# Expert pass of a two-layer trunk: two groups of 32 slots without a branch and the third under a condition, in place of one of four arms

## The chip, the cores and the metric

One core of a Trainium2 chip runs the whole program. The metric is the time of one execution on the device in microseconds (us).

## The reference

The reference is a trunk of two layers over 256 tokens of width 1024, all in float32. Each layer has a mixer (convolution and spatial gating) and a feed-forward part. The feed-forward part of layer 0 is dense; that of layer 1 sends every token to two of eight experts, and it is there that the change is made:

```python
def swiglu(h, wg, wu, wd):
    return jnp.einsum('...f,fd->...d', jax.nn.silu(h @ wg) * (h @ wu), wd)

def moe_swiglu(h, router, wg, wu, wd):
    ...
    top_vals, top_idx = lax.top_k(logits, TOP_K)
    gates = jax.nn.softmax(top_vals, axis=-1)
    ...
    for e in range(N_EXPERTS):
        out = out + dense_gate[:, e:e + 1] * swiglu(ht, wg[e], wu[e], wd[e])
```

`h` is 256 x 1024, and each expert has `wg` and `wu` of 1024 x 2816 and `wd` of 2816 x 1024. A final RMS norm follows.

## The kernel before

**Stages.** `mixer(0)`, `dense`, `mixer(1)` and `moe` run one after the other; `moe` begins at about 393 us of the profiled execution. The routing is worked out at the end of `mixer(1)`: `rt.pos` holds for every token and expert its place among that expert's tokens (a large negative number where it is not sent there), `rt.icnt` the number of tokens of each expert.

**Slots.** An expert's tokens are gathered into slots, 128 in the main pass, in groups of `GW` = 32 (`NG` = 4). `one_hot` (L1184) compares `pos` with 0 to 127 for a pair of experts. `gather` (L1208) multiplies the normalised tokens `xn` by this one-hot matrix, so that `xg` has the chosen tokens as columns, for two experts at once. If an expert has more than 128 tokens, the whole pass is run once more (`second_half`, L1470) under a condition at the end (L1523), then with all four groups; in this execution it is not run.

**Sections.** Each expert's 2816 hidden columns are cut into three blocks: two of 1024 and one of 768. For each block `hidden` (L1264) computes gate and up projection, and `down` (L1327) multiplies by the rows of `wd`. A section is one call of `hidden` or `down`; `experts` (L1374) puts them in this order for expert e: hidden 0, down 2 of expert e-1, hidden 1, down 0, hidden 2, down 1. Between them stand `turn` (L1300: transposes of the hidden values into `ah`), `back` (L1341: transposes of the one-hot matrix into `pt`), `combine` (L1355: copies of `mpd` to `eo`, the products `pcomb` that bring slots back to tokens, and eight additions to `xs` on VectorE), and, after every second expert, the gather for the next pair.

**Matmuls of a section.** `side_by_side` (L1249) puts four matmuls beside each other on TensorE: the 32 slots of a group are the stationary operand, and four column ranges of the weights stream past them into four quarters of the PSUM partitions. All of L1253 in the profile is this function. A float32 matmul shows as two MATMUL and two LDWEIGHTS instructions. One group is 128 of these MATMUL instructions of 256 columns in hidden 0 and in hidden 1, 192 of 128 columns in hidden 2, 64 of 256 columns in down 0 and in down 1, and 48 in down 2.

**Branches.** How many groups an expert needs is known at run time only. `arms` (L1228) writes every section out four times, for one to four groups, and two nested conditions choose (L1233, L1234, L1239). The count `c` is loaded into a register of TensorE once for each expert (L1516). The instructions of the arms lie one behind the other in the order of the source: the then-arm follows its test, and at its end a jump leads over the else-arm. Groups that did not run get zeros in PSUM by one small matmul (`blank`, L1256), since the elementwise steps after it take all four.

**Loads.** The weights of the experts are 264 loads of 1 MB in the order of their use, into a ring of 19 buffers (L1198); an expert has 33: 8, 8 and 6 for the three blocks of `hidden`, 4, 4 and 3 for those of `down`. At the start of each section `upto` issues on SyncE's queue the loads whose buffers the sections before it have used; each waits there for the last matmul that reads its buffer.

Of the kernel before, what the change touches and what calls it, by code (L numbers as in the profile page):

```python
# [7 lines left out]
F32 = mybir.dt.float32  # L8
# [3 lines left out]
AF = mybir.ActivationFunctionType  # L12
OP = mybir.AluOpType
# [3 lines left out]
P = 128  # L17
# [16 lines left out]

NG = 4
GW = P // NG
CHUNKS = [(0, 512), (512, 512), (1024, 512), (1536, 512), (2048, 512), (2560, 256)]
# [216 lines left out]
def hybrid_trunk(  # L254
# [905 lines left out]
    class Route:  # L1160
# [20 lines left out]
        def one_hot_tile(self):  # L1181
            return self.pool.tile([P, NT, 2, P], F32, name="oh")

        def one_hot(self, oh, e0, t):  # L1184
            V.tensor_tensor(oh[:, t], iot[:, None, :].to_broadcast([P, 2, P]),
                            self.pos[:, t, e0:e0 + 2, None].to_broadcast([P, 2, P]), op=OP.is_equal)

    def moe(sg, rt):
        with ExitStack() as c2:
# [18 lines left out]
            def gather(e0):  # L1208

                xg = rt.pool.tile([P, KD, 2 * P], F32, name="xg", tag="big0") if e0 // 2 % 2 else pool.tile([P, KD, 2 * P], F32, name="xg")  # L1210
                oh = rt.oh

                def part(k2, ps, eng):
                    for q in range(2):
                        k = k2 * 2 + q
                        for t in range(NT):
                            T.matmul(ps[:, q * 256:(q + 1) * 256], xn[:, t, k * P:(k + 1) * P],
                                     oh[:, t].rearrange("p e s -> p (e s)"), start=(t == 0), stop=(t == NT - 1))
                    copy(eng, xg[:, k2 * 2:k2 * 2 + 2].rearrange("p k s -> p (k s)"), ps)
                return xg, [lambda new, eng, k2=k2: part(k2, new(), eng) for k2 in range(KD // 2)]  # L1220
# [6 lines left out]

            def arms(c, body):  # L1228

                if c is None:  # L1230
                    body(NG)
                    return
                with tc.If(c > 2 * GW) as more:  # L1233
                    with tc.If(c > 3 * GW) as most:  # L1234
                        body(4)
                    with most.Else():
                        body(3)
                with more.Else():
# [9 lines left out]

            def side_by_side(banks, w, n, x_, first, last, srcs):  # L1249

                for g in range(n):
                    for q in range(4):
                        T.matmul(region(banks, w, g, q), x_(g, q), srcs[q], start=first and g % (512 // w) == 0, stop=last,  # L1253
                                 skip_group_check=True)

            def blank(banks, w, n):  # L1256

                m = 512 // w
                for b, bank in enumerate(banks):
                    k = min(max(n - b * m, 0), m)  # L1260
                    if k < m:
                        T.matmul(bank[:, k * w:], zero[:, :P], zero[:, :512 - k * w], start=(k == 0), stop=True, skip_group_check=True)

            def hidden(e, b, xg, c):  # L1264
# [13 lines left out]

                def body(n):
                    def x_(k):  # L1280
                        return lambda g, q: xg[:, k, o + g * GW:o + (g + 1) * GW]
                    nl = 4 * w // 256
                    for j in range(2):
                        for k in range(KD):
                            side_by_side(banks[j], w, n, x_(k), k == 0, k == KD - 1, [cols(nl * j, k, 4 * w, q * w, w) for q in range(4)])
                        blank(banks[j], w, n)
                    if both:
                        for k in range(KD):
                            side_by_side(both, P, n, x_(k), k == 0, k == KD - 1, [cols(2 * nl + q // 2, k, 256, q % 2 * P, P) for q in range(4)])
                        blank(both, P, n)  # L1290
                arms(c, body)
                h = pool.tile([P, 2, 512], F32, name="sg")
                for i in range(nb):
                    A.activation(h[:, i], banks[0][i], AF.Silu)  # L1294
                    V.tensor_tensor(h[:, i], h[:, i], banks[1][i], op=OP.mult)  # L1295
                if both:
                    A.activation(h[:, 1], both[0], AF.Copy)
                return h

            def turn(b, h, between=None):  # L1300
# [4 lines left out]
                for i in range(2):  # L1305
                    ps = tr_tile()
                    for j in range(4):
                        T.transpose(ps[:, j * P:(j + 1) * P], h[:, i, j * P:(j + 1) * P], ident)  # L1308
                    if b == 2 and i == 1:

                        v = ps.rearrange("p (g q s) -> p g q s", g=NG, q=4)
                        o = a[:, 1, :256].rearrange("p (g q s) -> p g q s", g=NG, q=2)
                        A.activation(o, v[:, :, :2], AF.Silu)  # L1313
                        V.tensor_tensor(o, o, v[:, :, 2:], op=OP.mult)  # L1314
                    else:
                        copy(V if i else A, a[:, i], ps)

# [9 lines left out]
            def down(e, b, x_, pd, c):  # L1327
# [3 lines left out]

                def body(n):
                    for blk in range(2 * len(ids)):
                        row = raws[blk // 2][:, blk % 2 * D:(blk % 2 + 1) * D]
                        side_by_side(pd, 256, n, lambda g, q: x_(blk, g), b == 0 and blk == 0, b == 2 and blk == 2 * len(ids) - 1,
                                     [row[:, q * 256:(q + 1) * 256] for q in range(4)])
                    if b == 0:
                        blank(pd, 256, n)
                arms(c, body)

            def back(e):  # L1341

                pt = pool.tile([P, NG, NT, P], F32, name="pt")
                for b in range(2):
                    ps = tr_tile("ppt")
                    for i in range(2):
                        for t in range(NT):
                            g = 2 * b + i
                            for q in range(4):
                                T.matmul(ps[q * GW:(q + 1) * GW, (i * NT + t) * P:(i * NT + t + 1) * P],  # L1350
                                         rt.oh[:, t, e % 2, g * GW:(g + 1) * GW], ident, start=True, stop=True)
                    copy(A, pt[:, 2 * b:2 * b + 2].rearrange("p g t s -> p (g t s)"), ps)
                return pt

            def combine(e, pd, pt):  # L1355

                eo = pool.tile([P, 2, 512], F32, name="eo", tag="ah", bufs=2)
                for b in range(2):
                    copy(V if b else A, eo[:, b], pd[b])
                yield  # L1360
# [210 lines left out]
```

## Time and profile before

| | us |
|---|---|
| median of 3 runs | 1656.04 |
| lowest and highest of them | 1649.04, 1656.56 |
| the profiled execution | 1650.51 |
| its span, first to last instruction | 1648.8 |
| TensorE busy with matmuls in the span | 1167.5 (71%) |
| VectorE, ScalarE, GpSimd busy | 331.9, 286.9, 144.0 |

The page of the profile has the busy time of each engine and its share in 40 slices of the span. Its windows give the same for any stretch, with TensorE's granted clock (1.00 is full speed) and the share of time in which the 16 DMA engines were busy. The timeline lists instructions in order of time, with the idle time of the engine ahead of each in brackets and what ended it. A busy time of 1167.5 us doesn't say that TensorE was at its peak in it. Branches are not counted as busy; they are run by TensorE's sequencer, which issues its instructions, and the answer for a source line gives their durations.

### The profile page before, as it was taken

Reading aid. Unit: us, or ns where it says so; the run is one execution under the profiler, and the core shown is the slowest. Engines: PE = TensorE matmul, PEld = TensorE weight load, DVE = VectorE, ACT = ScalarE, POOL = GpSimd, SP = SyncE. Lnnn points to the kernel's source line nnn. Section 1 sums busy time; section 2 is a strip of 40 time slices with the busy share of each in tenths; the row PEclk is TensorE's granted clock in tenths of the full one; section 3 lists DMA queues with packets and bytes.
Section 4 is the critical chain, followed back from the end, with each engine's and each line's share of the span. In section 5 each row is a group of like instructions: output and inputs, shape, how many; then the busy total and the mean of one; then the engine's idle time right before and its main releaser. Section 6 shows DMA issues by size and latency. Waiting matters only on the chain. (4 is left out here: it accounts for less than half of the span.)

```text
span 1648.8 us, 33006 instructions
## 1 busy us (share of the span) xinstructions
PE 1167.5 (71%) x15191; PEld 828.1 (50%) x15201; DVE 331.9 (20%) x641; ACT 286.9 (17%) x474; POOL 144.0 (9%) x115
## 2 busy tenths in 40 slices
PE   7899999997546466675657685556666768475765
PEld 7678888876233344343434553353334535353443
DVE  6955554792100100010001001000010001000101
ACT  5754444672000001000000000000000100000001
POOL 4820000682000000000000000000000000000001
PEclk8999999998767788797879897877787989778787
DMA  8555555643875576545465745652643543736440
GB/s 333 204 179 190 181 183 185 246 169 155 333 288 201 235 310 245 216 172 219 194 268 235 310 161 227 261 204 105 254 185 157 236 197 136 284 157 238 165 155 30
DMA packets 52134, 346.21 MB, mean 210 GB/s; under 512 B 6596, under 2 KB 8444, under 8 KB 11388
## 3 DMA queue, kind: packets, MB, share of 16 engines
q1 hardware_dynamic: 48876, 339.40, 52.4%
q8 instruction: 274, 4.49, 1.2%
q10 hardware_dynamic: 2960, 2.13, 0.5%
q14 instruction: 24, 0.20, 0.0%
HBM read 340.46 MB, written 1.05 MB: 207 GB/s over the span
## 5 line engine op out<-in xcount | busy, mean ns | idle before, releaser
L1253 PE MATMUL mpd<-wraw,ah 128*32 128x256 f32 x3344 | 235.6, 445 | 204.4 <-issue 141.1
L1253 PE MATMUL pg<-wraw,xg 128*32 128x256 f32 (+1 forms) x3648 | 219.2, 405 | 152.6 <-issue 137.1
L1253 PEld LDWEIGHTS mpd<-wraw,ah 128*32 128x32 f32 x3344 | 129.6, 127 | 304.9 <-issue 233.6
L1253 PEld LDWEIGHTS pg<-wraw,xg 128*32 128x32 f32 x3648 | 136.8, 130 | 233.4 <-issue 183.0
L1253 PE MATMUL pu<-wraw,xg 128*32 128x256 f32 (+1 forms) x3648 | 170.6, 346 | 0.8 <-issue 0.8
L1253 PEld LDWEIGHTS pu<-wraw,xg 128*32 128x32 f32 x3648 | 111.1, 111 | 53.5 <-issue 1.7
L314 ACT ACTIVATE whi<-wraw 128x1024 fp32r<-128x1024 f32 x110 | 116.4, 1059 | 118.9 <-PE pd L375 31.1
L1295 DVE TENSOR_TENSOR sg<-sg,pu 128x512 f32<-128x512 f32 x40 | 26.1, 685 | 545.4 <-PE pu L1253 344.1
L1436 POOL TENSOR_TENSOR wraw<-xs,wraw 128x512 f32<-128x512 f32 (+1 forms) x4 | 3.9, 1001 | 1244.0 <-DVE xs L1371 1244.0
L1294 ACT ACTIVATE sg<-pg 128x512 f32<-128x512 f32 x40 | 22.2, 595 | 517.4 <-PE pu L1253 353.6
L319 DVE TENSOR_TENSOR wlo<-wraw,whi 128x1024 fp32r<-128x1024 f32 x73 | 89.5, 1226 | 86.2 <-ACT whi L314 84.6
L319 POOL TENSOR_TENSOR wlo<-wraw,whi 128x1024 fp32r<-128x1024 f32 x37 | 89.2, 2428 | 14.0 <-ACT whi L314 13.1
L823 DVE SCALAR_TENSOR_TENSOR acc<-big,cwt,acc 128x256 f32<-128x256 f32 x199 | 86.8, 482 | 1.7
L1226 ACT ACTIVATE ah<-ptr 128x512 f32<-128x512 f32 x24 | 14.3, 597 | 343.4 <-issue 192.5
L1350 PE MATMUL ppt<-ident,oh 128*32 128x128 f32 x512 | 28.6, 395 | 50.9 <-issue 50.9
L1308 PE MATMUL ptr<-ident,sg 128*128 128x128 f32 x192 | 30.0, 304 | 31.8 <-issue 31.1
L1350 PEld LDWEIGHTS ppt<-ident,oh 128*32 128x32 f32 x512 | 22.8, 160 | 55.0 <-issue 53.8
L1224 DVE COPY ah<-ptr 128x512 f32<-128x512 f32 x16 | 11.1, 692 | 194.0 <-PE ptr L1308 194.0
L1308 PEld LDWEIGHTS ptr<-ident,sg 128*128 128x128 f32 x192 | 23.9, 155 | 39.3 <-issue 37.8
L1314 DVE TENSOR_TENSOR ah<-ah,ptr 128x256 f32<-128x256 f32 x8 | 3.4, 422 | 200.1 <-ACT ah L1313 200.1
L756 PE MATMUL mm<-xh,whi 128*128 128x256 f32 x128 | 37.6, 293 | 4.4 <-ACT whi L314 4.4
L1253 PE MATMUL pgu<-wraw,xg 128*32 128x128 f32 x1216 | 35.6, 274 | 2.4 <-issue 2.4
(226 smaller groups left out, 1428.6 us busy)
## 6 DMA issues: line engine op xcount, KB each, us to landing
wraw<-in_blocks_dram SPq DMA_DIRECT2D x316, 1024.0 KB, 9.4
wraw<-in_blocks_dram SPq DMA_DIRECT2D x10, 512.0 KB, 11.1
xs<-in_x_dram SPq DMA_DIRECT2D x2, 512.0 KB, 8.1
wst<-in_sgu_w_dram ACTq DMA_DIRECT2D x2, 256.0 KB, 15.7
grow<-in_norm_ffn_dram ACTq DMA_DIRECT2D x2, 256.0 KB, 3.3
wraw<-in_norm_final_dram SPq DMA_DIRECT2D x1, 512.0 KB
out_dram<-wraw SPq DMA_DIRECT2D x4, 128.0 KB, 2.7
out_dram<-wraw SPq DMA_DIRECT2D x2, 256.0 KB
```

The costliest lines, as they stand in the source:

```text
L314: A.activation(ready[i][0][:, :w], src, AF.Copy)
L319: eng.tensor_sub(ready[i][1][:, :w], src, ready[i][0][:, :w].bitcast(F32))
L756: T.matmul(o, hi[:, ws], xt[0][:, k], start=(k == 0), stop=False)
L823: V.scalar_tensor_tensor(accp, src, wv, accp if w else pa, op0=OP.mult, op1=OP.add)
L1224: V.tensor_copy(o, i)
L1226: A.activation(o, i, AF.Copy)
L1253: T.matmul(region(banks, w, g, q), x_(g, q), srcs[q], start=first and g % (512 // w) == 0, stop=last, skip_group_check=True)
L1294: A.activation(h[:, i], banks[0][i], AF.Silu)
L1295: V.tensor_tensor(h[:, i], h[:, i], banks[1][i], op=OP.mult)
L1308: T.transpose(ps[:, j * P:(j + 1) * P], h[:, i, j * P:(j + 1) * P], ident)
L1350: T.matmul(ps[q * GW:(q + 1) * GW, (i * NT + t) * P:(i * NT + t + 1) * P], rt.oh[:, t, e % 2, g * GW:(g + 1) * GW], ident, start=True, sto ...
L1436: G.tensor_tensor(y[:, t, pieces[j]], xs[:, t, pieces[j]], gain[:, pieces[j]], op=OP.mult)
```

## The change

Two groups of 32 slots are worked off for every expert ahead of any branch. One condition follows, `c > 64`: the third group, or, in the else-arm, the zeros for it. The main pass has 96 slots, 32 fewer: the one-hot matrix, the gather, the transposes in `turn` and `back`, the copies and the combination cover three groups instead of four. An expert with more than 96 tokens would be dealt with by `further`, with up to two more passes under conditions at the end. The loop of a section changes with it: before, all groups of a weight block ran one after the other, then the next block; now the first two groups run over all blocks of the section, and after the condition the third group runs over all of them again. The loads, their order and their buffers stay as they are.

```diff
-NG = 4
-GW = P // NG
+NG = 3
+GW = 32
+SL = NG * GW
...
-            return self.pool.tile([P, NT, 2, P], F32, name="oh")
+            return self.pool.tile([P, NT, 2, SL], F32, name="oh")
 
         def one_hot(self, oh, e0, t):
-            V.tensor_tensor(oh[:, t], iot[:, None, :].to_broadcast([P, 2, P]),
-                            self.pos[:, t, e0:e0 + 2, None].to_broadcast([P, 2, P]), op=OP.is_equal)
+            V.tensor_tensor(oh[:, t], iot[:, None, :SL].to_broadcast([P, 2, SL]),
+                            self.pos[:, t, e0:e0 + 2, None].to_broadcast([P, 2, SL]), op=OP.is_equal)
...
-                            T.matmul(ps[:, q * 256:(q + 1) * 256], xn[:, t, k * P:(k + 1) * P],
+                            T.matmul(ps[:, q * 2 * SL:(q + 1) * 2 * SL], xn[:, t, k * P:(k + 1) * P],
                                      oh[:, t].rearrange("p e s -> p (e s)"), start=(t == 0), stop=(t == NT - 1))
-                    copy(eng, xg[:, k2 * 2:k2 * 2 + 2].rearrange("p k s -> p (k s)"), ps)
+                    copy(eng, xg[:, k2 * 2:k2 * 2 + 2].rearrange("p k s -> p (k s)"), ps[:, :4 * SL])
...
-            def arms(c, body):
-
+            def arms(c, body, blank):
+
+                body(range(NG - 1))
                 if c is None:
-                    body(NG)
+                    body((NG - 1,))
                     return
-                with tc.If(c > 2 * GW) as more:
-                    with tc.If(c > 3 * GW) as most:
-                        body(4)
-                    with most.Else():
-                        body(3)
-                with more.Else():
-                    with tc.If(c > GW) as two:
-                        body(2)
-                    with two.Else():
-                        body(1)
+                with tc.If(c > (NG - 1) * GW) as full:
+                    body((NG - 1,))
+                with full.Else():
+                    blank()
 
             def region(banks, w, g, q):
 
                 m = 512 // w
                 return banks[g // m][q * GW:(q + 1) * GW, g % m * w:(g % m + 1) * w]
 
-            def side_by_side(banks, w, n, x_, first, last, srcs):
-
-                for g in range(n):
+            def side_by_side(banks, w, gs, x_, first, last, srcs):
+
+                for g in gs:
                     for q in range(4):
                         T.matmul(region(banks, w, g, q), x_(g, q), srcs[q], start=first and g % (512 // w) == 0, stop=last,
                                  skip_group_check=True)
 
-            def blank(banks, w, n):
-
-                m = 512 // w
-                for b, bank in enumerate(banks):
-                    k = min(max(n - b * m, 0), m)
-                    if k < m:
-                        T.matmul(bank[:, k * w:], zero[:, :P], zero[:, :512 - k * w], start=(k == 0), stop=True, skip_group_check=True)
+            def blank(banks, w):
+
+                b, o = divmod((NG - 1) * w, 512)
+                T.matmul(banks[b][:, o:o + w], zero[:, :P], zero[:, :w], start=(o == 0), stop=True, skip_group_check=True)
...
-                o = e % 2 * P
+                o = e % 2 * SL
                 w = 256 if b < 2 else 128
-                nb = 4 * w // 512
+                nb = -(-NG * w // 512)
...
-                def body(n):
+                def body(gs):
                     def x_(k):
                         return lambda g, q: xg[:, k, o + g * GW:o + (g + 1) * GW]
                     nl = 4 * w // 256
                     for j in range(2):
                         for k in range(KD):
-                            side_by_side(banks[j], w, n, x_(k), k == 0, k == KD - 1, [cols(nl * j, k, 4 * w, q * w, w) for q in range(4)])
-                        blank(banks[j], w, n)
+                            side_by_side(banks[j], w, gs, x_(k), k == 0, k == KD - 1, [cols(nl * j, k, 4 * w, q * w, w) for q in range(4)])
                     if both:
                         for k in range(KD):
-                            side_by_side(both, P, n, x_(k), k == 0, k == KD - 1, [cols(2 * nl + q // 2, k, 256, q % 2 * P, P) for q in range(4)])
-                        blank(both, P, n)
-                arms(c, body)
+                            side_by_side(both, P, gs, x_(k), k == 0, k == KD - 1, [cols(2 * nl + q // 2, k, 256, q % 2 * P, P) for q in range(4)])
+
+                def blanks():
+                    for v in banks:
+                        blank(v, w)
+                    if both:
+                        blank(both, P)
+                arms(c, body, blanks)
...
+                    m = NG if b == 2 else min(4, 2 * NG - 4 * i)
+                    for j in range(m):
                        T.transpose(ps[:, j * P:(j + 1) * P], h[:, i, j * P:(j + 1) * P], ident)
...
-                def body(n):
+                def body(gs):
                     for blk in range(2 * len(ids)):
                         row = raws[blk // 2][:, blk % 2 * D:(blk % 2 + 1) * D]
-                        side_by_side(pd, 256, n, lambda g, q: x_(blk, g), b == 0 and blk == 0, b == 2 and blk == 2 * len(ids) - 1,
+                        side_by_side(pd, 256, gs, lambda g, q: x_(blk, g), b == 0 and blk == 0, b == 2 and blk == 2 * len(ids) - 1,
                                      [row[:, q * 256:(q + 1) * 256] for q in range(4)])
-                    if b == 0:
-                        blank(pd, 256, n)
-                arms(c, body)
+                arms(c, body, (lambda: blank(pd, 256)) if b == 0 else lambda: None)
...
-                    for i in range(2):
+                    m = min(2, NG - 2 * b)
+                    for i in range(m):
...
-            def second_half():
-                V.tensor_scalar(pos, pos, -128.0, None, op0=OP.add)
+            def further():
+                V.tensor_scalar(pos, pos, -float(SL), None, op0=OP.add)
...
-            with tc.If(cnt > P):
-                second_half()
+            with tc.If(cnt > SL):
+                further()
+                with tc.If(cnt > 2 * SL):
+                    further()
```

## Rows read from the trace of the kernel before

**Rows 1.** The page, part 2: busy tenths of TensorE in 40 slices of the span.

```profile
PE   7899999997546466675657685556666768475765
```

**Rows 2.** Windows: stretch, its length, busy us (instructions) by engine, clock, DMA share, GB/s.

```profile
core 0: us, PE busy (x) PEld busy (x) DVE busy (x) ACT busy (x) POOL busy (x), PEclk, DMA share, GB/s
20.00:60.00 40.00, 37.87 (x251) 34.11 (x250) 37.32 (x74) 26.45 (x46) 32.48 (x19) 0.99 0.97 404
...
393.00:1634.00 1241.00, 792.82 (x13261) 515.08 (x13270) 75.49 (x157) 66.55 (x119) 0.00 (x0) 0.81 0.54 215
403.00:500.00 97.00, 40.79 (x604) 24.29 (x605) 7.34 (x24) 5.96 (x11) 0.00 (x0) 0.72 0.77 300
...
714.00:718.00 4.00, 3.79 (x36) 2.04 (x40) 0.00 (x0) 0.00 (x0) 0.00 (x0) 0.50 0.02 4
727.00:737.00 10.00, 10.00 (x188) 6.05 (x192) 0.00 (x0) 1.09 (x2) 0.00 (x0) 1.00 0.46 171
...
1018.00:1041.00 23.00, 22.71 (x381) 13.32 (x385) 0.00 (x0) 1.09 (x2) 0.00 (x0) 0.91 0.19 74
```

**Rows 3.** Waits of TensorE's matmuls: total us, times, longest.

```profile
PE mpd L1253 <- issue: 141.1, 25, 18.1
...
PE mpd L1253 <- DMA wraw<-in_blocks_dram: 63.2, 5, 13.5
```

**Rows 4.** Branches by source line, whole span, then single ones: ns min/median/max, start us.

```profile
L1233 PEldq COMPARE_BRANCH  x48: 65/1720/7607, 399.7 to 1619.8; - x48
...
L1234 PEldq COMPARE_BRANCH  x48: 302/6192/8117, 654.7 to 1538.0; - x48
...
L1234 PEldq COMPARE_BRANCH  x1: 6619/6619/6619, 736.0 to 736.0; - x1
...
L1234 PEldq COMPARE_BRANCH  x1: 8117/8117/8117, 742.9 to 742.9; - x1
...
L1239 PEldq COMPARE_BRANCH  x1: 6515/6515/6515, 534.0 to 534.0; - x1
...
L1239 PEldq COMPARE_BRANCH  x1: 317/317/317, 894.5 to 894.5; - x1
...
L1239 PEldq COMPARE_BRANCH  x1: 5937/5937/5937, 621.1 to 621.1; - x1
...
L1239 PEldq COMPARE_BRANCH  x1: 3854/3854/3854, 1602.4 to 1602.4; - x1
...
L1239 PEldq COMPARE_BRANCH  x1: 316/316/316, 650.1 to 650.1; - x1
```

**Rows 5.** Timeline: start us, duration us, instructions, idle time before and its end.

```profile
393.76 8.97 PE L1217 MATMUL pgat<-oh,xn 128*128 128x256 f32 x32 [0.49 <-DVE cnt L1049]
...
489.21 1.96 PE L1350 MATMUL ppt<-ident,oh 128*32 128x128 f32 x64
...
703.94 1.09 PE L1308 MATMUL ptr<-ident,sg 128*128 128x128 f32 x8
...
726.93 10.57 PE L1253 MATMUL pu<-wraw,xg 128*32 128x256 f32 x192
...
751.19 12.85 PE L1253 MATMUL mpd<-wraw,ah 128*32 128x256 f32 x192 [13.48 <-DMA wraw<-in_blocks_dram]
...
783.39 5.45 PE L1253 MATMUL pu<-wraw,xg 128*32 128x128 f32 x192
...
957.23 3.72 PE L1217 MATMUL ptr<-oh,xn 128*128 128x256 f32 x16 [0.31 <-ACT ah L1226]
...
1100.48 0.56 PE L1253 MATMUL pgu<-wraw,xg 128*32 128x128 f32 x5 [2.18 <-issue]
...
1629.93 3.74 PE L1366 MATMUL pcomb<-eo,pt 32*128 32x256 f32 x64 [0.76 <-ACT eo L1226]
1633.69 3.23 DVE L1371 SCALAR_TENSOR_TENSOR xs<-pcomb,gate,xs 128x256 f32<-128x256 f32 x8 [3.76 <-PE pcomb L1366]
```

More of the change, by code (lines that the diff above doesn't have):

```diff
@@ L1208, in gather @@
             def gather(e0):
-                xg = rt.pool.tile([P, KD, 2 * P], F32, name="xg", tag="big0") if e0 // 2 % 2 else pool.tile([P, KD, 2 * P], F32, name="xg")
+                xg = rt.pool.tile([P, KD, 2 * SL], F32, name="xg", tag="big0") if e0 // 2 % 2 else pool.tile([P, KD, 2 * SL], F32, name="xg")
                 oh = rt.oh
@@ L1284, in body @@
                         for k in range(KD):
-                            side_by_side(banks[j], w, n, x_(k), k == 0, k == KD - 1, [cols(nl * j, k, 4 * w, q * w, w) for q in range(4)])
-                        blank(banks[j], w, n)
+                            side_by_side(banks[j], w, gs, x_(k), k == 0, k == KD - 1, [cols(nl * j, k, 4 * w, q * w, w) for q in range(4)])
                     if both:
                         for k in range(KD):
-                            side_by_side(both, P, n, x_(k), k == 0, k == KD - 1, [cols(2 * nl + q // 2, k, 256, q % 2 * P, P) for q in range(4)])
-                        blank(both, P, n)
-                arms(c, body)
+                            side_by_side(both, P, gs, x_(k), k == 0, k == KD - 1, [cols(2 * nl + q // 2, k, 256, q % 2 * P, P) for q in range(4)])
[5 more added lines that the diff above has]
+                arms(c, body, blanks)
                 h = pool.tile([P, 2, 512], F32, name="sg")
                 for i in range(nb):
-                    A.activation(h[:, i], banks[0][i], AF.Silu)
-                    V.tensor_tensor(h[:, i], h[:, i], banks[1][i], op=OP.mult)
+                    n = min(512, NG * w - 512 * i)
+                    A.activation(h[:, i, :n], banks[0][i][:, :n], AF.Silu)
+                    V.tensor_tensor(h[:, i, :n], h[:, i, :n], banks[1][i][:, :n], op=OP.mult)
                 if both:
-                    A.activation(h[:, 1], both[0], AF.Copy)
+                    A.activation(h[:, 1, :NG * P], both[0][:, :NG * P], AF.Copy)
                 return h
@@ L1306, in turn @@
                     ps = tr_tile()
-                    for j in range(4):
+                    m = NG if b == 2 else min(4, 2 * NG - 4 * i)
+                    for j in range(m):
                         T.transpose(ps[:, j * P:(j + 1) * P], h[:, i, j * P:(j + 1) * P], ident)
                     if b == 2 and i == 1:
-                        v = ps.rearrange("p (g q s) -> p g q s", g=NG, q=4)
-                        o = a[:, 1, :256].rearrange("p (g q s) -> p g q s", g=NG, q=2)
+                        v = ps[:, :NG * P].rearrange("p (g q s) -> p g q s", g=NG, q=4)
+                        o = a[:, 1, :NG * 2 * GW].rearrange("p (g q s) -> p g q s", g=NG, q=2)
                         A.activation(o, v[:, :, :2], AF.Silu)
@@ L1315, in turn @@
                     else:
-                        copy(V if i else A, a[:, i], ps)
+                        copy(V if i else A, a[:, i, :m * P], ps[:, :m * P])
                 def x_(blk, g):
@@ L1351, in back @@
                                          rt.oh[:, t, e % 2, g * GW:(g + 1) * GW], ident, start=True, stop=True)
-                    copy(A, pt[:, 2 * b:2 * b + 2].rearrange("p g t s -> p (g t s)"), ps)
+                    copy(A, pt[:, 2 * b:2 * b + m].rearrange("p g t s -> p (g t s)"), ps[:, :m * NT * P])
                 return pt
@@ L1358, in combine @@
                 for b in range(2):
-                    copy(V if b else A, eo[:, b], pd[b])
+                    n = min(512, 256 * NG - 512 * b)
+                    copy(V if b else A, eo[:, b, :n], pd[b][:, :n])
                 yield
```

## Prediction

> **What bounds the kernel now.** I read the slices of the page first [rows 1]: TensorE is busy nine tenths and more until about 400 us, and from there to the end only six to seven tenths. The second part is the expert pass, and only that is touched by the diff. The windows give its size [rows 2]: from 393 to 1634 us TensorE works for 792.82 of 1241 us, so it stands still for 448 us, and its granted clock is 0.81 on the mean. The DMA share there is 0.54, with 215 GB/s, while the first 60 us of the same run show that 404 GB/s are to be had. So neither the matmuls nor the loads fill this part.
>
> The list of waits names what TensorE waits for [rows 3]: mostly "issue", that is nothing that the profile knows of. The second row there puts 63 us down to loads, but not rightly, as the branches show. Asked by source line, they answer what the waits do not [rows 4]: the 48 jumps out of a then-arm at L1234 have a median of 6.2 us, and L1233, the outer test, takes between 65 ns (the program goes straight on) and 7.6 us (it jumps). The one wait of 13.48 us ahead of `mpd` at 751.19 [rows 5], which is among the five given to the loads, is two jumps one behind the other: 6.6 us from 736.0, out of the three-group arm of `hidden`, and 8.1 us from 742.9, over the four-group arm of `down` [rows 4]. They reach from 736.0 to 751.0. The loads were not late there: a window that begins a little later in another three-group section has TensorE at 22.71 of 23 us with the DMA at 0.19, that is with the ring of 19 loads full and waiting for buffers [rows 2]. So the pass is bound by its matmuls **and** by TensorE's own sequencer, which after every far jump has to get new code first. [...]
>
> The number of matmuls in a section of the timeline tells the groups that ran: 64 instructions of one tile for each group. The eight experts ran 1, 2, 3, 2, 3, 3, 3 and 2 groups, 19 in all. The arm for four never ran.
>
> **The change, part by part.**
>
> *Fewer and shorter jumps.* Every section now has two groups ahead of any branch, then one test. Going straight on into the third group costs some 70 ns by the least of L1233 [rows 4]. At its end the jump skips only one to three small matmuls, or nothing; I take 0.3 us, the price of the shortest jumps there are now (316 ns over one group of `down`, 64 matmul instructions and their weight loads) [rows 4]. The four experts that ran one or two groups do not take the third and jump over it. One group is 128 matmul instructions in blocks 0 and 1 of `hidden`, 192 in block 2, and 64, 64 and 48 in the blocks of `down`. The same distances are jumped today at the end of a two-group arm (L1239, over the one-group arm): over 128 there are six such jumps between 317 and 6515 ns, with a mean of 2.7 us; over 192 three between 3854 and 5937 ns, mean 4.9 [rows 4]. Over 64 and 48 I take the 0.3. That gives 4 x (2 x 2.7 + 4.9 + 3 x 0.3) = 45 us, and 24 x 0.3 = 7 us for the other four experts: **52 us** where 448 us are lost today. Bounds: 4 x 6 x 0.3 + 7 = 14 us, and 4 x (3 x 6.5 + 0.9) + 7 = 89 us.
>
> [...]
>
> *One group more.* Expert 0 has 25 rows and ran one group; it will run two, 20 in all. The price of a group at full clock: 192 matmul instructions of 256 columns (a float32 matmul is two) in 10.57 us, so 55 ns each, and 192 of 128 columns in 5.45 us, 28.4 ns each [rows 5]. One group has 128 + 128 in blocks 0 and 1, 64 + 64 + 48 in `down`, that is 432 x 55 = 23.8 us, and 192 x 28.4 = 5.45 us in block 2: 29.25 us. **20 x 29.25 = 585 us.** The added one is 29 us of it, and nothing hides it: it is in the sum. I take full clock for all of them, since the cause of the half clock, a stop of 5 to 13 us ahead of each section, goes for most; where TensorE was busy for 37.87 of 40 us it had 0.99 [rows 2].
>
> *96 slots for 128.* A quarter less of the gather, of the one-hot transposes (`back`), of the turns and of the combination. The gather of the first pair goes from 8.97 us to 6.7 [rows 5]; it began at 393.76, so with its last copy the first expert can begin at about **401.3** (now 411.25). Per expert: three turns 3 x 0.75 x 1.09 = 2.5; combination 0.75 x 3.74 = 2.8; `back` 0.75 x 1.96 = 1.5 [rows 5]; 6.8 in all. After the combination block 1 needs PSUM banks that VectorE still reads: eight additions in 3.23 us [rows 5]. Today a jump lies over that. Uncovered it costs between two of the eight (0.9 us) and all with the hand-over (3.5); nothing in the code demands all, but one wait may stand for several, so I take 2.3. That is 9.1 per expert, **73 us** in all. The gathers for the three later pairs: 3 x 2 x 0.75 x 3.72 = 16.7, and 1.5 us each for waits, an estimate from the 0.31 which that row shows and a last copy that no jump covers any more: **21 us** [rows 5]. The smaller copies on ScalarE and VectorE lie beside matmuls and change nothing in the sum.
>
> *Later releases.* A load's buffer is free when its last reader is through. With the third group behind the test that is the end of the section. Two of the rows above bound what that costs: 264 loads of 1 MB are 277 MB, 19 of them are under way or there when the pass begins, and the remaining 257 MB at 404 GB/s [rows 2] are through at 403 + 636 = 1039 us, ahead of the matmuls. So I put it at nothing; what covers it is the ring, which is full when the pass begins. A two-group expert uses up its 33 loads in 29.25 x 2 + 9 + 11 = 79 us, 2.4 us each, and one takes 2.6 to come: the ring is eaten up slowly there, by some 7 us an expert, and the three-group experts give it back.
>
> *Stops inside straight code.* The row of 22.71 busy of 23 us is 381 matmul instructions with hardly a stop [rows 2]; against it stands one such as the 2.18 us inside block 2 at 1100.48 [rows 5]. Between nothing and 2 us in each of the 48 sections is 0 to 96 us; I take **20**, nearer to the first, as most bodies show none.
>
> **Sum.** 401 + 585 + 73 + 21 + 52 + 20 = 1152 us to the last combination. From there to the end the program is as it was: from 1633.67 (end of the last `pcomb` [rows 5]) to 1648.8, 15 us. That makes a span of 1167 against 1648.8. The profiled execution took 1650.5 in all, 1.7 more than its span; the median of the runs was 5.5 us above it. I add 7 and round up: **1180 us**, 29% less.
>
> **The rivals.**
>
> *The loads become the bound.* In the stretch from 403 to 500 us, with expert 0 using its data fast, 300 GB/s were moved [rows 2]. Were that the most that this order of releases gives, 257 MB would take 857 us: 403 + 857 + 10 for what is left of the matmuls + 15 = 1285 us. For it: the later releases, and that the pass would use its data 1.6 times as fast. Against: that stretch too is full of jumps, and 404 GB/s were held over 40 us. In a mild form it is inside the range.
>
> *It does not do what it says: the test itself stops the sequencer.* If every section still lost 6.2 us at its one branch (the median of L1234), 48 x 6.2 = 298 us would take the place of 52: some 1425 us. Against it is the least of L1233, 65 ns, for the same kind of test when it falls through.
>
> *Straight code is fetched too slowly.* This is the one that ends slower than before. A jump over 64 matmul instructions is nearly free and one over 192 is not [rows 4], so what the sequencer has at hand ends between; say it is 128. The 20 groups are 20 x 624 = 12480 of them, 98 such pieces. If each were fetched only when the last is used up, it would cost what a far jump does, 6.2 us: 98 x 6.2 = 608 us more, 1115 + 608 = 1720 us. The point from which it decides is a fetch that lasts longer than a piece: 128 x 55 ns = 7 us, and 3.6 us in block 2. The row of 23 us speaks against it; for block 2, with the DMA busier than now, it may hold in part: 30 pieces by 2.6 us are 78 us, which the range has.
>
> **How the numbers follow.** The forecast as worked out has 0.80; the loads as the bound, or a test that still stops, beyond 1300 us: 0.13; a time under the range 0.03; no change 0.01; straight code too slow, slower than before, 0.03. The low end takes the lower bounds of jumps, inner stops and the wait for VectorE: 1180 - 38 - 20 - 11 = 1111, and since not all of them will be at their best, 1125. The high end takes in the upper bounds, 37 for the jumps and 76 for the inner stops, 1293, and the bound by loads, 1285: 1300. So 1125 to 1300, with the likeliest case inside it. A measurement of this kernel tells 0.5% from no change, and faster by more than that holds in all cases but the last two: 0.96, with 0.01 for the same and 0.03 for slower.
>
> **What the profile after would show.** Branches at the one test with 0.1 to 0.3 us in experts 2, 4, 5 and 6, and 0.3 to 6 us in experts 0, 1, 3 and 7; 20 groups, so 3520 matmul instructions into `mpd`; granted clock of the pass near 0.95; idle time of TensorE under 150 us there; a DMA share near 0.85. I would be wrong if the gaps ahead of the sections remain (second rival), if TensorE waits ahead of `pg` or `mpd` with the DMA share at 1 (first rival), or if stops are spread within the bodies (third).

## The result and the profile after

The changed kernel took 1194.68 us (median of 3 runs, 1189.93 to 1198.35), against 1656.04 before: a ratio of 0.722, with a 95% interval of 0.717 to 0.727. The forecast was 1180 us, within 1125 to 1300. The profiled execution is the slowest of the three, 1198.35 us with a span of 1196.6.

The slices of the page of the kernel after (TensorE's busy tenths, its granted clock, the DMA share), to be held against [rows 1]:

```profile
PE   8999999999999986986998997799799889989884
...
PEclk9999999999999887998999998999999999999998
DMA  8934455454843599999699789978969966888951
```

The expert pass begins in the fourteenth slice and is now nearly as full as the dense part. Windows of the kernel after, with the columns of [rows 2]; the first is the whole pass:

```profile
392.00:1182.00 790.00, 696.59 (x13552) 477.72 (x13552) 63.70 (x158) 57.16 (x119) 0.00 (x0) 0.95 0.83 335
...
841.00:864.00 23.00, 15.31 (x539) 14.29 (x531) 0.03 (x1) 0.55 (x2) 0.00 (x0) 1.00 1.00 403
578.00:640.00 62.00, 60.87 (x1105) 37.16 (x1108) 6.29 (x14) 3.65 (x7) 0.00 (x0) 1.00 0.84 343
```

The pass takes 790 us in place of 1241 [rows 2]. TensorE stands still for 93 us of it (448 before), and its matmuls take 697 us, where a smaller number took 793: the granted clock is 0.95 and was 0.81. The loads come at 335 GB/s, 215 before, and fill 0.83 of the DMA engines' time.

The waits of TensorE's matmuls in the kernel after (total us, times, longest), to be held against [rows 3]; L1249 is `side_by_side`, L1255 the zeros that follow a jump over the third group, L1235 the one test:

```profile
PE pg L1255 <- issue: 23.5, 6, 5.6
PE pu L1249 <- issue: 19.4, 9, 2.9
PE pgu L1249 <- issue: 12.4, 8, 2.8
PE mpd L1249 <- issue: 7.9, 5, 3.6
PE pg L1249 <- DVE xs L1370: 6.7, 7, 1.0
PE pg L1249 <- issue: 5.8, 6, 2.2
PE ppt L1348 <- issue: 5.6, 3, 3.2
PE ptr L1307 <- PEq L1235: 3.3, 7, 1.9
...
PE mpd L1255 <- issue: 2.6, 1, 2.6
```

Three kinds are to be seen. After jumps: the two rows of L1255 and that of L1235, 29 us. Within straight code: `pu`, `pgu`, `mpd`, `pg` and `ppt`, 51 us; by the timeline some 37 of them lie inside block 2 of `hidden`, and most of the other 14 a little way behind a jump or behind block 2. For VectorE: 6.7 us. No load is among them. The one branch line of the kernel after, with the columns of [rows 4]:

```profile
L1235 PEldq COMPARE_BRANCH  x72: 65/176/6107, 412.3 to 1176.3; - x72
```

Half of its 72 branches take under 0.18 us; all 72 together take 50.8 us in the sequencer. In the timeline after, a section with three groups runs through its test without a gap (no bracket), while block 2 of `hidden` stops every 128 matmul instructions:

```profile
609.43 7.11 PE L1249 MATMUL pg<-wraw,xg 128*32 128x256 f32 x128 [0.95 <-DVE xs L1370]
616.36 7.09 PE L1249 MATMUL pu<-wraw,xg 128*32 128x256 f32 x128
623.27 3.64 PE L1249 MATMUL pg<-wraw,xg 128*32 128x256 f32 x64
626.72 3.64 PE L1249 MATMUL pu<-wraw,xg 128*32 128x256 f32 x64
630.17 10.54 PE L1249 MATMUL mpd<-wraw,ah 128*32 128x256 f32 x192
...
842.49 1.49 PE L1249 MATMUL pu<-wraw,xg 128*32 128x128 f32 x47
845.49 2.48 PE L1249 MATMUL pu<-wraw,xg 128*32 128x128 f32 x81 [1.51 <-issue]
847.70 1.49 PE L1249 MATMUL pgu<-wraw,xg 128*32 128x128 f32 x47
851.98 2.48 PE L1249 MATMUL pgu<-wraw,xg 128*32 128x128 f32 x81 [2.79 <-issue]
```

### The profile page after: what moved, and what is told of

It reads as the page before. It is cut to its first block, busy times and chain, and to the rows that moved or that the text cites. A ratio compares the mean times of both kernels' runs of the same rounds, so it can differ in the third digit from the quotient of the medians.

```text
span 1196.6 us, 33425 instructions
## 1 busy us (share of the span) xinstructions
PE 1072.5 (90%) x15484; PEld 791.6 (66%) x15484; DVE 319.6 (27%) x641; ACT 277.5 (23%) x474; POOL 143.9 (12%) x115
## 5 line engine op out<-in xcount | busy, mean ns | idle before, releaser
L1249 PE MATMUL mpd<-wraw,ah 128*32 128x256 f32 x3520 | 208.1, 393 | 8.3 <-issue 7.9
L1249 PE MATMUL pu<-wraw,xg 128*32 128x256 f32 (+1 forms) x3840 | 189.2, 351 | 19.4 <-issue 19.4
L1249 PE MATMUL pg<-wraw,xg 128*32 128x256 f32 (+1 forms) x3840 | 183.8, 345 | 12.4 <-DVE xs L1370 6.7
L1249 PEld LDWEIGHTS mpd<-wraw,ah 128*32 128x32 f32 x3520 | 124.3, 114 | 86.0 <-issue 22.3
L1249 PEld LDWEIGHTS pu<-wraw,xg 128*32 128x32 f32 x3840 | 124.7, 113 | 76.9 <-issue 22.3
L1249 PEld LDWEIGHTS pg<-wraw,xg 128*32 128x32 f32 x3840 | 118.2, 110 | 71.9 <-issue 10.8
L1293 DVE TENSOR_TENSOR sg<-sg,pu 128x512 f32<-128x512 f32 (+2 forms) x40 | 21.7, 554 | 447.0 <-ACT sg L1292 236.8
L1292 ACT ACTIVATE sg<-pg 128x512 f32<-128x512 f32 (+2 forms) x40 | 19.6, 490 | 473.5 <-PE pg L1255 143.8
L1249 PE MATMUL pgu<-wraw,xg 128*32 128x128 f32 x1280 | 44.0, 288 | 12.4 <-issue 12.4
L1249 PEld LDWEIGHTS pgu<-wraw,xg 128*32 128x32 f32 x1280 | 39.8, 117 | 14.6 <-issue 14.5
L759 PE MATMUL mm<-xh,wlo 128*128 128x256 f32 x128 | 36.5, 285 | 0.5 <-DVE wlo L320 0.5
L343 PE MATMUL pu<-whi,xh 128*128 128x512 f32 (+1 forms) x96 | 36.5, 381 | 0.0
L758 PE MATMUL mm<-xl,whi 128*128 128x256 f32 x128 | 36.5, 285 | 0.0
L343 PE MATMUL pg<-whi,xh 128*128 128x512 f32 (+1 forms) x96 | 36.2, 377 | 0.0
L344 PE MATMUL pg<-wlo,xh 128*128 128x512 f32 (+1 forms) x96 | 36.1, 376 | 0.0
```

What stands on the lines that cost most here:

```text
L343: T.matmul(bank, xs_[0][:, c, sl], w, start=first, stop=False)
L344: T.matmul(bank, xs_[0][:, c, sl], lo, start=False, stop=False)
L758: T.matmul(o, hi[:, ws], xt[1][:, k], start=False, stop=False)
L759: T.matmul(o, lo[:, ws], xt[0][:, k], start=False, stop=(k == KD - 1))
L1292: A.activation(h[:, i, :n], banks[0][i][:, :n], AF.Silu)
L1293: V.tensor_tensor(h[:, i, :n], h[:, i, :n], banks[1][i][:, :n], op=OP.mult)
```

## The experiments

The theory: the time before went with far jumps of TensorE's sequencer, and with the slow clock behind them; what is left after is jumps in the four experts that skip the third group, and code that comes late in block 2 of `hidden` because the loads take the DMA engines it comes by. The rivals: that the smaller slots did a good part; that the loads hold the pass; that code cannot come faster in any case. All times are medians of 4 runs, beside 7 runs of the kernel before on the same chip (1657 and 1658 us); the changed kernel's 1194.68 us is the median of 3 runs above. The new order of the loop in a section was not tried by itself: it stands in all versions but the one with three arms. Idle time is the length of the pass, from the first gather to the last combination, less the busy time of TensorE's matmuls, in the window that is shown.

**Straight code with 128 slots.** `NG = 4`, and:

```diff
-                body(range(NG - 1))
+                body(range(2))
...
-                with tc.If(c > (NG - 1) * GW) as full:
-                    body((NG - 1,))
+                with tc.If(c > 2 * GW) as full:
+                    body((2,))
+                    blank(3)
                 with full.Else():
-                    blank()
+                    blank(2)
+                    blank(3)
```

> The straight code alone, with the 128 slots of before: two groups ahead of the branch, the third under the condition, zeros for the fourth. If the time went with the jumps, only what the 32 slots cost comes back: per expert three turns by 0.27 us, the combination 0.9 and the one-hot transposes 0.5, so 2.2 x 8 = 18 us, and four gathers by 1.9 us, 8 us: about 1220 us. If the smaller slots carry a large part of the gain, 1300 us or more.

Measured: 1232.07 us, ratio to before 0.744 (0.740 to 0.747). Window of the pass:

```profile
396.00:1215.00 819.00, 720.86 (x13920) 497.72 (x13920) 76.39 (x154) 67.25 (x119) 0.00 (x0) 0.96 0.80 323
```

The idle time is 98 us, close to the 93 of the changed kernel. Of the 461 us that the change brought, 424 come with the straight code alone, and the 32 slots are worth 37, where the expectation had 26: 24 of them are more matmul time (721 for 697 us), 4 a later beginning of the pass. The first rival falls.

**96 slots with three arms.** In place of the straight groups and the one test:

```diff
+                with tc.If(c > 2 * GW) as more:
+                    body(range(3))
+                with more.Else():
+                    with tc.If(c > GW) as two:
+                        body(range(2))
+                    with two.Else():
+                        body(range(1))
```

> The 96 slots alone: three arms chosen ahead of everything, as before with four. By the jumps: 24 sections with three groups jump out over the two other arms (6.2 us each, 149), 18 sections with two groups jump in (112) and out over one group (34), 6 sections with one group jump twice (74): 369 us of the 484 us of branches before. The same share of the 354 us of idle time and of the clock lost beside it: some 330 us above the changed kernel, less 29 us for the group that expert 0 does not run: about 1500 us. If the slots or a smaller program were what counts: 1250 to 1300 us.

Measured: 1481.54 us, ratio 0.895 (0.891 to 0.899). Window of the pass:

```profile
393.00:1462.00 1069.00, 745.05 (x12937) 490.02 (x12936) 62.17 (x156) 56.81 (x119) 0.00 (x0) 0.84 0.63 249
```

324 us of idle time are there again, and the slow clock (0.84). The branches take 329 us in the sequencer, against 488 in the kernel before and 51 in the changed kernel. So the 175 us that this version gains over the kernel before are not the worth of 96 slots, which the experiment before puts at 37; an arm less is also fewer and shorter jumps. Both experiments say that the larger part of the gain is the code in a straight line.

**A far jump more in every section**, in the changed kernel:

```diff
+                if c is not None:
+                    with tc.If(c > 250):
+                        body(range(NG))
                 body(range(NG - 1))
```

> The changed kernel with one far jump more in each of the 48 sections: a copy of the three groups stands ahead of the section under a condition that never holds, and is jumped over (384, 384, 576, 192, 192 and 144 matmul instructions). By the price of such jumps in the kernel before, 6.2 us, 48 of them are 298 us in the sequencer; 378 of 488 us showed there as idle time, so 230 to 300 us, and 1.5 us of slow clock behind each, 70 us: 1500 to 1560 us. If far jumps are not what cost the time before, it stays below 1300 us.

Measured: 1484.64 us, ratio 0.898 (0.893 to 0.903). The branch line that was added, and the pass:

```profile
L1232 PEldq COMPARE_BRANCH  x48: 340/6010/8433, 398.0 to 1451.0; - x48
```

```profile
392.00:1466.00 1074.00, 772.51 (x13552) 519.88 (x13552) 63.10 (x157) 57.06 (x119) 0.00 (x0) 0.86 0.62 248
```

The same 13552 matmul instructions, with 208 us more of idle time and 76 us more of busy time at a lower clock: 284 us for 48 jumps, 5.9 us each, all told. This is a net price. At the added jumps themselves (stops that begin at most 2.5 us behind one) TensorE stands still for 246 us, inside the 230 to 300 of the expectation; what the expectation left out, and why it was 15 to 75 us too high, is that other stops go: at `pu` and `pgu`, 31.8 us in the changed kernel, 1.9 us are left.

**No branch at all.** Three groups for every expert:

```diff
-                with tc.If(c > (NG - 1) * GW) as full:
-                    body((NG - 1,))
-                with full.Else():
-                    blank()
+                body((NG - 1,))
```

> No branch in the main pass: all three groups of every expert are worked off. Four groups more than in the changed kernel are 4 x 29.25 = 117 us; what its nine long jumps cost (28 us of idle time, and the slow clock behind them) goes; block 2 of hidden, which runs into late code, gets four groups longer, 5 to 10 us: about 1275 us. If the test or the jump at the end of an arm costs more than the 0.07 and 0.18 us that their rows show, it is the less for it: 1230 us or below.

Measured: 1244.01 us, ratio 0.751 (0.747 to 0.756), 49 us above the changed kernel, between the two expectations. Window of the pass:

```profile
394.00:1228.00 834.00, 783.18 (x16012) 543.98 (x16016) 63.57 (x156) 57.75 (x119) 0.00 (x0) 0.99 0.79 317
```

Four groups more cost 87 us of matmul time and not 117, and 43 us of idle time go. The clock says why: 0.99 here, 0.95 in the changed kernel. So about 30 us of the changed kernel's 697 are slow clock; 24 groups of 29.25 us and the 78 us of gathers, turns and the rest that the forecast has beside them make 780. No cost of the test itself is to be seen: the idle time that goes is that of the jumps (29 us), and 11 of the 51 us of stops in straight code.

**One group first in expert 0:**

```diff
-                body(range(NG - 1))
+                n = 1 if e == 0 else NG - 1
+                body(range(n))
...
-                with tc.If(c > (NG - 1) * GW) as full:
+                with tc.If(c > n * GW) as full:
+                    body(range(n, NG))
```

> Expert 0 works off one group ahead of the branch and has two under the condition; the other experts are as in the changed kernel. One group less is 29 us less of matmuls. Its six jumps now go over two groups (256, 256, 384, 128, 128 and 96 matmul instructions): by the distance rule of the traces the first three cost some 6 us and two of the others 3 to 5, about 27 us against some 8 us today: 1180 to 1190 us, so little or no gain. If the distance of a jump does not matter, 1165 us.

Measured: 1188.95 us, ratio 0.718 (0.714 to 0.721), which overlaps with that of the changed kernel: no difference can be told. Window of the pass:

```profile
393.00:1176.00 783.00, 672.23 (x12936) 459.51 (x12936) 62.95 (x154) 57.10 (x119) 0.00 (x0) 0.94 0.84 338
```

The matmul time falls by 24 us, the idle time rises by 17. So the group that expert 0 runs for nothing costs about what the jumps over it would.

**No loads after the first ring.** Sections beyond the first 19 loads read what the ring holds, so 245 of the 264 loads, and with them the right weights, are left out:

```diff
+            if j >= rest["load"] + RAW_BUFS + MORE_RAW + LATE_RAW:
+                rawof[j] = rawof[j - RAW_BUFS - MORE_RAW - LATE_RAW]
+            else:
                 place(j)
                 load_raw(j)
```

> The changed kernel without loads after the first 19 of the expert pass (later sections read what the ring holds; this leaves 245 of the 264 loads out). If the stops inside block 2 of hidden are code that is fetched too slowly beside the loads, they go and with them the slow clock after them: 1195 - 50 - 20 = about 1125 us. If the fetch of code is too slow by itself, or 16 KB cannot come faster than in 6 us, the stops stay and the time is 1185 to 1195 us. If TensorE is held back by the loads themselves, it falls below 1110 us and the gaps that go are ahead of sections.

Measured: 1106.01 us, ratio 0.668 (0.665 to 0.671), 89 us under the changed kernel. Its pass, and block 2 of an expert with three groups in its timeline:

```profile
394.00:1091.00 697.00, 666.97 (x13552) 456.02 (x13552) 62.95 (x154) 57.23 (x119) 0.00 (x0) 0.99 0.03 11
```

```profile
608.34 3.70 PE L1252 MATMUL pg<-wraw,xg 128*32 128x128 f32 x128
611.86 3.68 PE L1252 MATMUL pu<-wraw,xg 128*32 128x128 f32 x128
615.35 3.68 PE L1252 MATMUL pgu<-wraw,xg 128*32 128x128 f32 x128
618.84 1.93 PE L1252 MATMUL pg<-wraw,xg 128*32 128x128 f32 x64
```

Not one stop is left inside block 2, so code can come as fast as it is used there, and it is the loads beside it that make it late. The idle time falls from 93 to 30 us, the matmul time by 30 us with the clock at 0.99. The time is below the 1110 us that I had set for "held back by the loads themselves", but the gaps that went are not ahead of sections: they are stops inside straight code and the far jumps, which became shorter too (the longest is 3977 ns where the changed kernel had 6107). My 1125 had left the jumps as they were, and had taken 20 us for the slow clock, where 30 went.

The trace shows the code itself. Among the DMA queues there is one of the kind "instruction" (packets, MB, share of the 16 engines), first of the kernel before, then of the changed kernel:

```profile
q8 instruction: 274, 4.49, 1.2%
...
q8 instruction: 143, 2.34, 0.8%
```

Each of its packets is 16 KB, in straight code one for 128 matmuls with their 128 weight loads, and each of the 36 stops of 0.4 us and more that the pass of the changed kernel has with "issue" ends 1.3 to 1.6 us after such a packet has landed. Inside `hidden` the next packet starts 3.6 us after the matmuls go on (median of 22 stops) and takes 1.0 us; with some 1.5 us from its landing to the next matmul a piece of code takes 6.1 us, where 128 matmuls with 128 columns take 3.5. Without the loads a packet takes no less (143 packets for 0.9% of the 16 engines' time in a span of 1103.6 us, so 1.1 us each): beside them it is late because it starts late.

**Block 2 with 256 columns.** Gate in two quarters of the PSUM partitions, up in the other two:

```diff
-                    for j in range(2):
+                    for j in range(2 if b < 2 else 0):
...
                     if both:
                         for k in range(KD):
+                            side_by_side(wide, 256, gs, x_(k), k == 0, k == KD - 1, [cols(nl * (q // 2), k, 512, q % 2 * 256, 256) for q in range(4)])
+                        for k in range(KD):
                             side_by_side(both, P, gs, x_(k), k == 0, k == KD - 1, [cols(2 * nl + q // 2, k, 256, q % 2 * P, P) for q in range(4)])
...
+                    A.activation(h[:, 0], wide[0], AF.Copy)
+                    V.tensor_copy(h[:, 1, :256], wide[1][:, :256])
+                    A.activation(h[:, 2, :NG * P], both[0][:, :NG * P], AF.Copy)
```

`turn` then does for all of block 2 what it did for its last 256 columns: SiLU and product after the transposes.

> Block 2 of hidden written with 256 columns: for the first 512 of its columns, gate in two quarters of the PSUM partitions and up in the other two, in place of two passes of 128 columns; 128 matmul instructions for a group in place of 192, the same columns, three transposes more per expert (0.4 us). If code comes too late there since the instructions are too short, most of the 50 us of stops inside block 2 and some 15 us of slow clock go: 1135 to 1145 us. If the code that is late in block 2 is late elsewhere then, since the loads take what the fetch needs anyway: 1175 to 1195 us.

Measured: 1156.94 us, ratio 0.698 (0.693 to 0.702), the fastest version here that uses the right weights. Its pass, and block 2 of an expert with three groups:

```profile
397.00:1142.00 745.00, 682.94 (x12292) 444.71 (x12291) 65.99 (x169) 59.80 (x127) 0.00 (x0) 0.97 0.87 355
```

```profile
636.46 7.11 PE L1249 MATMUL pg<-wraw,xg 128*32 128x256 f32 x128
643.39 3.46 PE L1249 MATMUL pgu<-wraw,xg 128*32 128x128 f32 x120
647.73 0.43 PE L1249 MATMUL pgu<-wraw,xg 128*32 128x128 f32 x8 [0.88 <-issue]
647.94 3.66 PE L1249 MATMUL pu<-wraw,xg 128*32 128x256 f32 x64
651.40 1.74 PE L1249 MATMUL pgu<-wraw,xg 128*32 128x128 f32 x56
654.04 0.43 PE L1249 MATMUL pgu<-wraw,xg 128*32 128x128 f32 x8 [0.90 <-issue]
```

In this expert the part with 256 columns has no stop (two others have one of 0.6 and one of 1.0 us there), and the one with 128 has short ones. 31 us of idle time and 14 us of matmul time go, 38 us of the whole; the pass began 4 us later in this execution. I had expected 50 to 60. The waits tell why it was less:

```profile
PE mpd L1249 <- issue: 14.3, 6, 4.1
...
PE pgu L1249 <- issue: 4.0, 6, 1.2
...
PE pu L1249 <- issue: 1.6, 2, 1.0
```

Of some 37 us of stops in block 2 less than 6 are left, but those in `mpd` rise from 7.9 to 14.3 us: part of the late code is late elsewhere then, as the second expectation had it.

**Loads in halves.**

```diff
-        cut = 1024 if h is not None or i + END_LOADS >= len(loads) else n
+        cut = 1024 if h is not None or i >= rest["load"] else n
```

> The changed kernel with every load of the expert pass issued as two of 512 KB, so that its rows are of 4 KB and not of 8. The bytes, their order and the buffers stay. If a piece of code waits on a DMA engine behind the row that is under way there, its wait is halved and some of the stops inside block 2 go: 1160 to 1175 us. If it waits behind all that is queued, or for its turn in any other way, nothing changes: 1190 to 1200 us, or a little more since SyncE issues twice as often.

Measured: 1207.98 us, ratio 0.731 (0.726 to 0.736), 13 us above the changed kernel, though the two intervals just touch, so that the loss is small if it is one: beyond what the second expectation named, and on the far side of the first. Window of the pass:

```profile
394.00:1190.00 796.00, 689.85 (x13552) 474.62 (x13552) 63.13 (x156) 57.16 (x119) 0.00 (x0) 0.96 0.87 333
```

The idle time is 106 us, 13 more than with whole loads. The next packet of code starts 3.7 us after the matmuls go on (median of the stops inside `hidden`), 3.6 with whole loads. So rows of half the length did not make its wait shorter here: the stops at `pu`, `pgu` and `pg` with "issue" are 48.3 us in all, for 37.6 with whole loads. What the code does wait for stays open.

## Why the prediction was right, point by point

**What bounds it.** Right, and shown from both sides: the straight code alone brings 424 of the 461 us, and 48 far jumps put back into the changed kernel have a median of 6.0 us in the sequencer, where L1234 had 6.2 [rows 4]. (The prediction calls all 48 branches of L1234 jumps out of an arm; only half are, and the other 24, such as the one at 742.9, lead over the four-group arm into the one for three.) That the 13.48 us ahead of `mpd` [rows 5] were not a load was read rightly as well: with more data per second, no wait for a load is left. And that TensorE's sequencer has to get new code shows in the trace of before: in its pass each of the 75 stops of 0.4 us and more with "issue" ends 1.3 to 2.3 us after a packet of the queue of the kind "instruction" has landed, and each of the six that are put down to loads of the experts' weights 1.6 to 2.4 us after one.

**The jumps.** Forecast 52 us, measured 29 us as idle time. The prediction took the sequencer's time for idle time: in the sequencer the branches take 50.8 us, but TensorE has matmuls left when a jump begins (the one at 461.45 takes 5.33 us, and TensorE works on until 462.31). That 50.8 is so near to 52 is luck: the eight jumps over 128 matmul instructions took 13 us where 22 were reckoned, the twelve over 64 and 48 took 10.5 for 3.6. The test that falls through takes 65 to 70 ns, as L1233 had said. Of the 24 sections that skip the third group, only nine had a branch of over 1 us, from 2.25 (at 523.9) to 6.11 (at 554.5): all four over 192, three of eight over 128, one of eight over 64 and one of four over 48. The distance alone does not decide it; this one leads over 64:

```profile
L1235 PEldq COMPARE_BRANCH  x1: 3985/3985/3985, 532.3 to 532.3; - x1
```

**The group for expert 0.** Forecast 29 us, found 24 us of matmul time, given back by the jumps that it saves.

**The 96 slots.** The pass began at 392.4 with the gather and its first section at 399.7, for 401.3 forecast. The wait for VectorE after the combination is 0.95 us an expert and not 2.3: TensorE waits for the first two of the eight additions. That is 12 us that I had too many.

**Later releases** cost nothing that can be seen: no matmul waits for a load. The first rival, the loads as the bound, is out in the form in which it was put (1285 us). Its true form is another: the loads hold up the code, and all that hangs on them is 89 us by the experiment without them.

**Stops inside straight code.** Here the sum was wrong by its size: 20 us taken, 51 measured. I took the lower part of 0 to 96 since most bodies of before showed none [rows 2]. But those ran with the DMA at 0.19, and the change itself brings the DMA to 0.83, to 1.00 in the window above in which block 2 runs. The third rival named the place and the cause (block 2, 78 us in part, "with the DMA busier than now"), and its point of decision was right too: a fetch that lasts longer than a piece, 7 us with 256 columns and 3.6 in block 2. Beside the loads a piece of code took 6.1 us. I should have taken it into the sum; 37 us lie in block 2, the rest behind it and behind jumps. The sections with 256 columns from 578 to 640 us had hardly a stop (60.87 of 62 us busy), and block 2 without loads had none. With loads it has them, and so have some sections with 256 columns: `mpd` stops five times, 7.9 us in all.

**The clock.** This step failed: I took full clock for all matmuls. Measured are 697 us where the forecast has 663 (585 for the groups, 78 for the rest), and the two runs at a clock of 0.99 bear those 663 out: 667 us with the same instructions and no loads. So some 30 us were missing. The prediction's own last part had the clock of the pass near 0.95, as it was; the sum did not charge for it. The cause that I named for the half clock (0.50 from 714 to 718 us [rows 2]), stops ahead of sections, went for most; but stops of up to 3.6 us inside them came in, jumps of up to 5.6 us stayed, and after one of them the matmuls are slow again: 108 instructions of `mpd` take 9.12 us after the 3.62 us at 434.78, with a granted clock of 0.50 from 435 to 440 us, where 128 take 7.11 without a stop, at 1.00 from 526 to 533:

```profile
434.78 9.12 PE L1249 MATMUL mpd<-wraw,ah 128*32 128x256 f32 x108 [3.62 <-issue]
...
526.64 7.11 PE L1249 MATMUL mpd<-wraw,ah 128*32 128x256 f32 x128
```

**The sum.** Jumps -23, wait for VectorE -12, beginning -2; stops +31, clock +30: 24 us of the 29 by which the last combination of the profiled execution (1181) is later than the forecast (1152). Of the rest 4 us are matmul time (34 us over the forecast, of which 30 are put down to the clock here), the remainder small waits. The forecast for the whole was 1.2% too low, and that it was so near is in part luck: two misses of 30 us in it were partly made good by two that went the other way, and the 7 us added to the span and the rounding up, 13 us together, covered nearly half of what was left.

## What to carry to other kernels

Look up the branches of the busiest engine by their source line before its waits are believed: a wait put down to "issue", or to a load that landed long ago, was here code that was being fetched, as the packets of the queue of the kind "instruction" showed (each of the 36 stops of 0.4 us and more with "issue" in the pass of the kernel after ended 1.3 to 1.6 us behind one). Work that nearly every case needs goes ahead of the branch, with a short and rare part behind it; a group of matmuls done for nothing (24 us) cost here no more than the jumps over it. When a change makes an engine busier, every row that was free of stops has to be read again at the new load of the DMA engines: here code came by a DMA queue too, and of the 51 us of stops in straight code 37 were in block 2 of `hidden`, with its short instructions.

## What the runs showed of the hardware

A jump over 48 or 64 matmul instructions and their weight loads took 0.2 to 0.8 us in the traces before and after, but once 3.5 and once 4.0; one over 128 between 0.3 and 6.5, one over 192 between 3.3 and 6.1, the added ones over three groups a median of 6.0. Of the 50.8 us of branches in the kernel after, 29 are idle time of TensorE. Behind a stop of 3.62 us there the granted clock was 0.50 (435 to 440 us), and with the 48 added jumps that of the pass was 0.86, where it had been 0.95. Code came as packets of 16 KB on a DMA queue of the kind "instruction" (143 of them in the kernel after, 274 in that before), in straight code one for 128 matmuls and their 128 weight loads; after a packet had landed it took 1.3 to 1.6 us in the kernel after until the matmuls went on. In straight code, instructions of 14 ns each came without a gap while the DMA engines were free (share 0.03, without expert loads), and with stops of 0.5 to 3 us, about one for 128 matmuls, while they were busy (1.00 from 841 to 864 us of the kernel after); the packet itself took 1.0 us beside the loads and 1.1 without them. Splitting the loads into rows of 4 KB for 8 did not make the packets of code start sooner (median 3.7 us for 3.6). Without expert loads the pass ran in 697 us, with TensorE busy for 667; the best version here with all loads lies about 50 us above that.
